# A hybrid decoder layer on one core: the SSM output in two parts, the pool fold in two kinds of PSUM banks, the norm weights first in the queue, the last rows by three engines

## The chip, the cores and the metric

The kernel runs on one core of one Trainium2 chip. The metric is the device time of one execution in microseconds. The core has a matrix engine (TensorE, PE), three other compute engines (VectorE or DVE, ScalarE or ACT, GpSimd or POOL) and a queue engine (SyncE, SP). All of them run their own instruction streams in order and wait for each other by semaphores. TensorE multiplies from SBUF into PSUM, which has eight banks here: two under the name mm and six under the name aux.

## The reference

One decoder layer: a normalised input goes through one projection, whose parts feed three mixers; each is gated, and an output projection with a norm is added to the input.

```python
h = rmsnorm(x, g_pre[i])                      # x: 2048 x 1024
proj = h @ w_in[i]                            # 1024 -> 2048
val, gate = proj[..., :MIX_W], proj[..., MIX_W:]
y_pool = pool_mixer(u_pool, w_pool[i], pool_scale[i])     # windows 2, 4, 8, 16; a 96x96 map per group
y_ssm = s5_mixer(u_ssm, ...)                  # 24 groups of 16 channels, 64 complex states each
y_att = memory_attention(q, mem, g_mem[i], w_kv[i])       # 4 heads, 256 memory tokens
y = jnp.concatenate([y_pool, y_ssm, y_att], axis=-1) * jax.nn.silu(gate)
out = y @ w_out[i]
x = x + rmsnorm(out, g_post[i])
```

The part of the state-space mixer that the change touches:

```python
bu = jnp.einsum('blgc,gnc->blgn', uf.astype(jnp.complex64), b_bar)
_, hs = lax.associative_scan(_ssm_combine, (lam_all, bu), axis=1)
y = jnp.einsum('blgn,gcn->blgc', hs, c_mat).real + d_skip.reshape(SSM_NG, SSM_GROUP) * uf
```

## The kernel before

All products are of float32 accuracy: each operand is split into a high and a low part (names ending in h and l), and a product is three matmuls (mm3, L163 to L165): high x high, high x low, low x high. The high part is a copy on ScalarE (L159), the low part a subtraction on VectorE or GpSimd (L160).

The run has these stages. Up to about 100 us x and the weights are loaded, the SSM input u is projected (pu) and stored, and keys and values of the memory are made. The rows of x are squared on ScalarE (L194, tile rs_x) and VectorE turns the sums into the norm factor rs_y (L170 to L198), which TensorE spreads to all partitions (rs_bc, L205). pool_fold multiplies the pool map into its columns of w_in ahead of use: eight pieces pf, each copied out by VectorE as wpo (L356) and stored; VectorE also copies out the projected u as us (L302). gpre, the norm weights, scales every split of x (L251, L252).

Then come two halves of the sequence, each with two chunks of 512 columns and 13 tasks (q, pool, gate): a task multiplies 128 columns of w_in with a chunk (pjq, pjp, pjg, L163 to L165) in an mm bank, and VectorE takes the product out times the norm factor (qf, up, gp). The first half runs from about 105 to 305 us, the second from about 345 to 505. Between them the splits of x for chunks 2 and 3 are made anew (xr is the load, xh and xl the split), and the weights that the first half has split are read back from DRAM (wq_h, wq_l and so on).

Between the tasks two queues of small steps are served, at a pace fixed by constants. One is the attention: scores psc, row maximum nb, exponentials pex, transposes ptp with their split pth and ptl, values po with lot and attn. The other is the SSM, in 12 blocks of two groups. For block b, ssm_build2 makes pr (a transpose, split into rh and rl) and pk (the short-range kernel, stored and read back as mraw, split into mh and ml). ssm_run1 multiplies the input (uh, ul) into pa, ScalarE swaps its halves (ax), VectorE and GpSimd rotate it (v), VectorE scans it (gg), rotates back (gs, h), and splits the states into hh and hl. ssm_run2 makes the output py of one aux bank: for each of two groups the near part, mh and ml times uh and ul, and the far part, oh and ol times hh and hl. ScalarE copies it out (ys) for the store. All these products sit in aux banks, and a new one has to wait until the reader of the bank's last content is done.

The order of instructions on each engine is set ahead of the run by a scheduler from the program's order and its own estimate of durations. From 505 us the GLU and the output projection (pout) run; the last 128 rows are done by out_last: three pieces of 512, 256 and 256 columns, squares on ScalarE, the reciprocal root oy on VectorE in small steps, the residual added in two halves (L1227), and a store on SP.

## Time and profile before

| | |
|---|---|
| median of the runs | 748.64 us (744.86, 748.64, 751.7) |
| profiled execution | 748.52 us, of which the span is 746.8 |
| mean granted clock of TensorE | 0.977 |
| TensorE busy | 711.5 us (95%) |
| VectorE busy | 498.8 us (67%) |
| ScalarE, GpSimd busy | 349.6 us, 354.0 us (47% each) |

The span is what the profiler's records cover; the rest of the time of the execution lies around it. Busy time is given for the whole span, and the stages differ much: a table of stages gives it for any stretch. A wait is the idle time of an engine ahead of an instruction, put down to what ended it. The granted clock is a share of TensorE's full clock of 2.4 GHz.

### The profile page before, as it was taken

What the parts mean: (1) busy time and instruction counts of PE and PEld (TensorE: products, weight loads), DVE (VectorE), ACT (ScalarE), POOL (GpSimd) and SP (SyncE); (2) the same over time, 40 slices, a digit from 0 to 9 for tenths busy, and PEclk for the clock granted to TensorE, in tenths of its full rate; (3) what the DMA queues carried; (4) which work ended last, traced back from release to release, by engine and by line L of the source; (5) the groups of instructions that cost most, each with busy time, mean ns of one, the idle gap of its engine ahead of it and who ended that gap; (6) DMA issues with size and microseconds to landing.
All of it is one profiled execution on the core that took longest, in us unless ns stands there. A gap on an engine that the chain in (4) does not pass through costs nothing.

```text
span 746.8 us, 10110 instructions
## 1 busy us (share of the span) xinstructions
PE 711.5 (95%) x3465; PEld 579.3 (78%) x3465; DVE 498.8 (67%) x865; ACT 349.6 (47%) x769; POOL 354.0 (47%) x311
## 2 busy tenths in 40 slices
PE   6999989998999799889999999999999999999996
PEld 5787768787878688667888888888877888888885
DVE  5699255689888887996887788648617963343324
ACT  5774662566565544354646555446633424121111
POOL 0058732768778476646948678103032621421121
PEclk9999989999999899899999999999999999999998
DMA  8998993333443366474232333387716453340331
GB/s 259 302 335 252 351 315 107 121 116 105 122 145 109 124 201 210 133 270 136 71 108 87 125 116 129 108 259 280 217 54 222 127 201 100 113 141 0 113 113 56
DMA packets 94978, 120.49 MB, mean 161 GB/s; under 512 B 31552, under 2 KB 62992, under 8 KB 94928
## 3 DMA queue, kind: packets, MB, share of 16 engines
q1 hardware_dynamic: 82032, 89.56, 37.8%
q10 hardware_dynamic: 12896, 30.30, 10.7%
q8 instruction: 27, 0.44, 0.2%
q14 instruction: 23, 0.19, 0.1%
HBM read 81.16 MB, written 38.68 MB: 160 GB/s over the span
## 4 chain that ended last, share of the span: by engine, by line
PE 67%; DVE 15%; DMA 8%; issue 4%; ACT 3%; POOL 2%; SPq 0%; ACTq 0%; DVEq 0%; POOLq 0%
PE pout L165 8%; PE pout L164 8%; PE pout L163 8%; PE pjg L163 6%; PE pjg L165 6%; PE pjg L164 6%; PE pz L163 2%; PE pz L164 2%; PE pz L165 2%; DMA xr<-in_xT_dram 2%; PE pjq L165 2%; PE pjq L163 2%; PE pjq L164 2%; DVE xl L252 2%; PE pjp L163 2%
## 5 line engine op out<-in xcount | busy, mean ns | idle before, releaser
L163 PE MATMUL pjg<-xh,wg_h 128*128 128x512 f32 x256 | 103.6, 405 | 0.0
L164 PE MATMUL pjg<-xl,wg_h 128*128 128x512 f32 x256 | 102.5, 400 | 0.0
L165 PE MATMUL pjg<-xh,wg_l 128*128 128x512 f32 x256 | 102.3, 400 | 0.0
L164 PE MATMUL pout<-wol,yh 128*128 128x512 f32 (+1 forms) x264 | 102.0, 386 | 0.0
L163 PE MATMUL pout<-woh,yh 128*128 128x512 f32 (+1 forms) x264 | 101.6, 386 | 0.0
L165 PE MATMUL pout<-woh,yl 128*128 128x512 f32 (+1 forms) x264 | 101.2, 387 | 0.0
L1213 POOL TENSOR_TENSOR ov<-ov,xres 128x1024 f32<-128x1024 f32 x15 | 36.7, 2446 | 127.6 <-DVE ov L1212 105.8
L1209 ACT ACTIVATE ov<-pout 128x512 f32<-128x512 f32 x30 | 17.9, 596 | 106.9 <-PE pout L165 83.9
L163 PEld LDWEIGHTS pjg<-xh,wg_h 128*128 128x128 f32 x256 | 48.7, 190 | 12.4 <-issue 1.2
L164 PEld LDWEIGHTS pout<-wol,yh 128*128 128x128 f32 x264 | 49.5, 188 | 10.9
L163 PEld LDWEIGHTS pout<-woh,yh 128*128 128x128 f32 x264 | 49.5, 188 | 10.9
L165 PEld LDWEIGHTS pout<-woh,yl 128*128 128x128 f32 x264 | 49.5, 188 | 10.9
L165 PEld LDWEIGHTS pjg<-xh,wg_l 128*128 128x128 f32 x256 | 48.7, 190 | 11.0
L164 PEld LDWEIGHTS pjg<-xl,wg_h 128*128 128x128 f32 x256 | 48.7, 190 | 10.5 <-issue 0.2
L160 POOL TENSOR_TENSOR yl<-yb,yh 128x512 fp32r<-128x512 f32 x20 | 27.2, 1395 | 59.4 <-ACT yh L159 59.4
L252 DVE SCALAR_TENSOR_TENSOR xl<-xr,gpre,xh 128x512 fp32r<-128x512 f32 x48 | 41.2, 874 | 16.4 <-ACT xh L251 15.8
L840 POOL TENSOR_TENSOR v<-v,ax 128x512 f32<-128x512 f32 x12 | 16.1, 1342 | 71.1 <-DVE ax L839 56.9
L251 ACT ACTIVATE xh<-xr,gpre 128x512 fp32r<-128x512 f32 x48 | 33.2, 714 | 26.5 <-DMA xr<-in_xT_dram 12.7
L163 PE MATMUL pu<-xh,wsh 128*128 128x512 f32 x96 | 38.5, 415 | 7.4 <-ACT wsh L159 5.9
L1181 DVE SCALAR_TENSOR_TENSOR ow<-ssq,ov 128x1 f32<-128x1 f32 x16 | 2.7, 168 | 55.5 <-ACT ov L1209 55.4
L163 PE MATMUL pjp<-xh,wp_h 128*128 128x512 f32 x96 | 38.7, 404 | 0.0
L164 PE MATMUL pu<-xl,wsh 128*128 128x512 f32 x96 | 38.4, 413 | 0.3 <-DVE xl L252 0.3
(299 smaller groups left out, 1915.0 us busy)
## 6 DMA issues: line engine op xcount, KB each, us to landing
xr<-in_xT_dram SPq DMA_DIRECT2D x32, 256.0 KB
rs_x<-in_x_dram SPq DMA_DIRECT2D x32, 256.0 KB
yd<-yt ACTq DMA_DIRECT2D x16, 512.0 KB
xres<-in_x_dram SPq DMA_DIRECT2D x16, 512.0 KB
out_dram<-ov SPq DMA_DIRECT2D x15, 512.0 KB
yb<-yd SPq DMA_DIRECT2D x20, 256.0 KB
wg_r<-in_w_in_dram SPq DMA_DIRECT2D x8, 512.0 KB
wsh<-wg_h ACTq DMA_DIRECT2D x8, 512.0 KB
```

Source lines behind the costliest of these rows:

```text
L160: sub.tensor_tensor(lo, src, hi.bitcast(F32), op=ALU.subtract)
L163: pe.matmul(ps, ahi, bhi, start=first, stop=False)
L164: pe.matmul(ps, ahi, blo, start=False, stop=False)
L165: pe.matmul(ps, alo, bhi, start=False, stop=last)
L251: act.activation(h, xr, AF.Copy, scale=gpre[:, k:k + 1])
L252: dve.scalar_tensor_tensor(l, xr, gpre[:, k:k + 1], h.bitcast(F32), op0=ALU.mult, op1=ALU.subtract)
L840: pool.tensor_tensor(v, v, ax, op=ALU.add)
L1181: dve.scalar_tensor_tensor(w, ssq[:, i:i + 1], 1.0 / D, v, op0=ALU.mult, op1=ALU.add)
L1209: act.activation(ov[:, HALVES[n]], ps[n], AF.Square, accum_out=ssq[:, n:n + 1])
L1213: pool.tensor_tensor(ov, ov, xr, op=ALU.add)
```

## The change

Four places are changed. The load of gpre is issued by SP instead of ScalarE, and stands first in SP's queue. The odd pieces of the pool fold go to aux banks, the even ones stay in mm banks. ssm_run2 is split: ssm_near stands where it stood, and ssm_far, with the copy ys and its stores, comes one step later, ahead of ssm_run1 of the next block; py stays open between them. The split of oh and ol goes along to the step of ssm_run1. In out_last the last two pieces are scaled by ScalarE, get the residual added on GpSimd and are stored by SP, and the first piece stays on VectorE and is stored from ScalarE's queue.

```diff
--- before.py
+++ after.py
@@ -139,7 +139,7 @@
 
 
     gpre = const.tile([P, KT], F32, name="gpre")
-    nc.scalar.dma_start(gpre, g_pre)
+    nc.sync.dma_start(gpre, g_pre)
     cs = const.tile([P, C_N], F32, name="cs")
     gmem = const.tile([P, KT], F32, name="gmem")
     warm = const.tile([P, 1], F32, name="warm")
@@ -349,7 +349,7 @@
                 dma(wt, w_in_poolT[:, :, r * P:(r + 1) * P])
 
                 def mms():
-                    ps = mm_bank(f"pf{r}", (P, POOL_W))
+                    ps = (aux_bank if r % 2 else mm_bank)(f"pf{r}", (P, POOL_W))
                     for g in range(4):
                         pe.matmul(ps[:, g * 96:(g + 1) * 96], wt[:, g, :], wp[:, g, :], start=True, stop=True)
                     wo = ev(f"wpo{r}", (P, POOL_W))
@@ -859,13 +859,19 @@
         split(hh, hl, h)
         o["hh"], o["hl"] = hh, hl
 
-    def ssm_run2(b, o):
+    def ssm_near(b, o):
+
+        py = o["py"] = aux_bank(f"py{b}", (P, 2, NJ))
+
+        for i in range(2):
+            mm3(py[:, i, :], o["mh"][:, i, :], o["ml"][:, i, :], o["uh"][:, i, :], o["ul"][:, i, :], i == 0, False)
+
+    def ssm_far(b, o):
+
         g0 = 2 * b
-        hh, hl = o["hh"], o["hl"]
-        py = aux_bank(f"py{b}", (P, 2, NJ))
+        hh, hl, py = o["hh"], o["hl"], o["py"]
         for i in range(2):
-            mm3(py[:, i, :], o["mh"][:, i, :], o["ml"][:, i, :], o["uh"][:, i, :], o["ul"][:, i, :], True, False)
-            mm3(py[:, i, :], o["oh"][:, i, :], o["ol"][:, i, :], hh[:, i, :], hl[:, i, :], False, True)
+            mm3(py[:, i, :], o["oh"][:, i, :], o["ol"][:, i, :], hh[:, i, :], hl[:, i, :], False, i == 1)
         ys = t2k(f"ys{b}", (P, 2, NJ))
         act.activation(ys, py, AF.Copy)
         for i in range(2):
@@ -878,20 +884,20 @@
         def call(*fs):
             def go():
                 for f, b in fs:
-                    if b < NB:
+                    if 0 <= b < NB:
                         f(b, ssm_state[b])
 
             ssm_q.append(go)
 
         call((ssm_input_load, 0), (ssm_build1, 0))
         call((ssm_build2, 0), (ssm_rotation, 0))
-        call((ssm_input_split, 0), (ssm_output_split, 0))
-        for b in range(NB):
+        call((ssm_input_split, 0))
+        for b in range(NB + 1):
             n = b + 1
-            call((ssm_run1, b), (ssm_kernel_load, b), (ssm_build1, n))
+            call((ssm_far, b - 1), (ssm_output_split, b), (ssm_run1, b), (ssm_kernel_load, b), (ssm_build1, n))
             call((ssm_kernel_split, b), (ssm_rotation, n))
             call((ssm_input_load, n))
-            call((ssm_run2, b), (ssm_build2, n), (ssm_input_split, n), (ssm_output_split, n))
+            call((ssm_near, b), (ssm_build2, n), (ssm_input_split, n))
 
 
     def q_split(ps, pr, c, qst):
@@ -1223,9 +1229,14 @@
             act.activation(sq[:, 0:cols.stop - cols.start], ps, AF.Square, accum_out=ssq[:, n:n + 1])
             dve.tensor_tensor(ov[:, cols], ps, w3["g"][:, cols], op=ALU.mult)
         r = out_rstd(c, tt, ssq, len(LAST))
-        for cols in HALVES:
-            dve.scalar_tensor_tensor(ov[:, cols], ov[:, cols], r, xr[:, cols], op0=ALU.mult, op1=ALU.add)
-            dma(out[rows, cols], ov[:, cols])
+        for cols in LAST[1:]:
+            st = t2k(f"st{cols.start}", (P, cols.stop - cols.start))
+            act.activation(st, ov[:, cols], AF.Copy, scale=r)
+            pool.tensor_tensor(st, st, xr[:, cols], op=ALU.add)
+            dma(out[rows, cols], st)
+        cols = LAST[0]
+        dve.scalar_tensor_tensor(ov[:, cols], ov[:, cols], r, xr[:, cols], op0=ALU.mult, op1=ALU.add)
+        store(out[rows, cols], ov[:, cols])
 
     HALVES = (slice(0, CH), slice(CH, D))
     LAST = (slice(0, CH), slice(CH, CH + 256), slice(CH + 256, D))
```

Behind line 860 the lines of the changed kernel are numbered 6 higher. What the change does to the order is shown at three places.

TensorE at SSM block 3, in the first half, before (pjg3_0_1 is a gate task on chunk 1, pr4 and pk4 belong to block 4):

```order
L165 MATMUL py3_2845<-hh3_2582,ol3_2498 128x256
L163 MATMUL py3_2845<-uh3_2493,mh3_2691 128x256
L164 MATMUL py3_2845<-ul3_2494,mh3_2691 128x256
L165 MATMUL py3_2845<-uh3_2493,ml3_2692 128x256
L163 MATMUL py3_2845<-hh3_2582,oh3_2497 128x256
L164 MATMUL py3_2845<-hl3_2583,oh3_2497 128x256
L165 MATMUL py3_2845<-hh3_2582,ol3_2498 128x256
L741 MATMUL pr4_2860<-ident_79,rt4_2594 128x128 x2
L163 MATMUL pjg3_0_1_2884<-xh1_4_860,wg3_0_h_2601 128x512
L164 MATMUL pjg3_0_1_2884<-xl1_4_861,wg3_0_h_2601 128x512
L165 MATMUL pjg3_0_1_2884<-xh1_4_860,wg3_0_l_2602 128x512
L750 MATMUL pk4_2867<-ox4_2589,rt4_2594 16x128 x2
```

and now, first the end of the near part with what follows it, then the far part:

```order
L163 MATMUL py3_2845<-uh3_2485,mh3_2691 128x256
L164 MATMUL py3_2845<-ul3_2486,mh3_2691 128x256
L165 MATMUL py3_2845<-uh3_2485,ml3_2692 128x256
L741 MATMUL pr4_2852<-ident_79,rt4_2592 128x128 x2
L750 MATMUL pk4_2859<-ox4_2587,rt4_2592 16x128 x2
L163 MATMUL pjg3_0_1_2872<-xh1_0_836,wg3_0_h_2599 128x512
L164 MATMUL pjg3_0_1_2872<-xl1_0_837,wg3_0_h_2599 128x512
```

```order
L165 MATMUL pjg3_0_1_2872<-xh1_7_878,wg3_0_l_2600 128x512
L163 MATMUL py3_2845<-hh3_2580,oh3_2551 128x256
L164 MATMUL py3_2845<-hl3_2581,oh3_2551 128x256
L165 MATMUL py3_2845<-hh3_2580,ol3_2552 128x256
L163 MATMUL py3_2845<-hh3_2580,oh3_2551 128x256
L164 MATMUL py3_2845<-hl3_2581,oh3_2551 128x256
L165 MATMUL py3_2845<-hh3_2580,ol3_2552 128x256
L163 MATMUL pa4_2930<-uh4_2868,rh4_2855 128x256
```

The six rows on hh, hl, oh and ol have moved 34 rows down, to just ahead of pa4, and pr4 and pk4 follow the near part directly. The attention's values po1_1_0 stand between the two pieces.

SP at the half change, where x is loaded anew and the split weights are read back, before:

```order
L116 DMA xr3_0_3536<-in_xT_dram 128x2x512
L116 DMA xr3_1_3546<-in_xT_dram 128x2x512
L116 DMA xr3_2_3560<-in_xT_dram 128x2x512
L116 DMA wq1_1_h_3548<-wsh1_1383 128x1024
L116 DMA wq1_1_l_3549<-wsl1_1384 128x1024
L116 DMA rs_b3_3580<-rsd_105 128x512
L116 DMA xr3_3_3570<-in_xT_dram 128x2x512
```

and now:

```order
L116 DMA xr3_0_3534<-in_xT_dram 128x2x512
L116 DMA xr3_1_3544<-in_xT_dram 128x2x512
L116 DMA wq1_1_h_3546<-wsh1_1379 128x1024
L116 DMA wq1_1_l_3547<-wsl1_1380 128x1024
L116 DMA rs_b3_3578<-rsd_105 128x512
L116 DMA xr3_2_3558<-in_xT_dram 128x2x512
L116 DMA xr3_3_3568<-in_xT_dram 128x2x512
```

The two tiles of wq1 have moved ahead of xr3_2, and xr3_2 stands behind them and rs_b3.

ScalarE from the output of block 0 to the swap ax of block 1, before:

```order
L159 ACTIVATE oh1_1743<-ox1_1487 128x256
L870 ACTIVATE ys0_1721<-py0_1708 128x512
L755 ACTIVATE kst1_1733<-pk1_1730 16x2x128
L934 ACTIVATE pex0_0_1_0_1673<-pex0_0_1_0_1673,ri0_0_1_0_1677 128x256 x2
L934 ACTIVATE pex0_0_1_1_1683<-pex0_0_1_1_1683,ri0_0_1_1_1687 128x256 x2
L964 ACTIVATE lot0_0_0_1769<-po0_0_0_1760 64x256
L119 DMA ysd_86<-ys0_1721 8x16x256 x2
L119 DMA kd1_1737<-kst1_1733 16x512
L997 ACTIVATE th0_0_1927<-gp0_0_1925 128x512
L964 ACTIVATE lot0_0_0_1769<-po0_0_0_1760 64x256
L831 ACTIVATE ax1_1806<-pa1_1799 64x512
L832 ACTIVATE ax1_1806<-pa1_1799 64x512
```

and now:

```order
L1003 ACTIVATE th0_0_1925<-gp0_0_1923 128x512
L970 ACTIVATE lot0_0_0_1757<-po0_0_0_1748 64x256
L876 ACTIVATE ys0_1791<-py0_1708 128x512
L831 ACTIVATE ax1_1804<-pa1_1797 64x512
L832 ACTIVATE ax1_1804<-pa1_1797 64x512
L119 DMA ysd_86<-ys0_1791 8x16x256
L970 ACTIVATE lot0_0_0_1757<-po0_0_0_1748 64x256
```

The copy ys0, which stood nine rows ahead of ax1, now stands directly ahead of it. In the same way ys1 to ys5 stand up to three rows ahead of ax2 to ax6, and there the split oh2 to oh6 stands next to them.

## Rows read from the trace of the kernel before

**Rows 1.** Table of stages: start:end us, length, busy us by engine, granted clock, DMA.

```profile
131.00:250.00 119.00, 111.51 (x611) 90.34 (x609) 101.08 (x142) 67.76 (x164) 91.80 (x77) 0.98 0.37 123
...
345.00:740.00 395.00, 392.85 (x1887) 321.14 (x1885) 230.34 (x446) 160.51 (x357) 150.74 (x119) 1.00 0.40 132
```

**Rows 2.** TensorE's waits over the whole run: us in total, times, longest.

```profile
PE py L164 <- DVE hl L160: 6.8, 5, 4.0
...
PE pf L354 <- DVE wpo L356: 4.7, 3, 3.2
...
PE pjq L163 <- DMA wq_h<-wsh: 2.0, 1, 2.0
...
PE py L163 <- ACT hh L159: 1.9, 1, 1.9
...
PE pjq L165 <- DMA wq_l<-wsl: 1.1, 2, 0.6
```

**Rows 3.** Timeline around the pool fold: start us, us, engine, line, operation.

```profile
98.69 1.03 DVE L302 COPY us<-pu 128x512 f32<-128x512 f32 x1 [6.71 <-ACT rs_x L194]
...
100.87 0.54 DVE L356 COPY wpo<-pf 128x384 f32<-128x384 f32 x1
...
105.39 0.77 PE L163 MATMUL pjq<-xh,wq_h 128*128 128x512 f32 x1
...
114.83 0.18 DVE L179 SCALAR_TENSOR_TENSOR rs_y<-rs_b,rs_y 128x16 f32<-128x16 f32 x1
...
117.17 1.05 PE L205 MATMUL rs_bc<-ident,rs_y 128*128 128x128 f32 x8
```

**Rows 4.** Table of stages, stretches with a low granted clock (PEclk).

```profile
101.20:108.00 6.80, 6.36 (x22) 5.64 (x23) 4.30 (x7) 5.25 (x17) 2.42 (x4) 0.50 1.04 386
...
212.60:217.30 4.70, 3.52 (x14) 2.96 (x13) 3.85 (x6) 1.87 (x7) 3.83 (x4) 0.64 0.10 41
...
246.60:254.80 8.20, 4.17 (x16) 3.25 (x16) 7.26 (x12) 3.30 (x9) 2.58 (x3) 0.58 0.51 185
...
309.40:316.30 6.90, 5.98 (x20) 4.58 (x19) 5.24 (x7) 1.87 (x4) 2.24 (x3) 0.51 0.58 181
```

**Rows 5.** Timeline, blocks 1, 2 and 3: ptl on VectorE, pk on TensorE.

```profile
181.38 1.29 DVE L160 TENSOR_TENSOR ptl<-ptp,pth 128x512 fp32r<-128x512 f32 x2
...
183.47 0.62 PE L750 MATMUL pk<-ox,rt 128*16 128x128 f32 x4
...
213.84 1.29 DVE L160 TENSOR_TENSOR ptl<-ptp,pth 128x512 fp32r<-128x512 f32 x2
...
217.46 0.62 PE L750 MATMUL pk<-ox,rt 128*16 128x128 f32 x4
...
251.29 1.29 DVE L160 TENSOR_TENSOR ptl<-ptp,pth 128x512 fp32r<-128x512 f32 x2
...
254.42 0.78 PE L750 MATMUL pk<-ox,rt 128*16 128x128 f32 x4
```

**Rows 6.** Timeline of ScalarE in block 0 and at the start of block 1.

```profile
155.71 0.61 ACT L870 ACTIVATE ys<-py 128x512 f32<-128x512 f32 x1
...
160.10 0.60 ACT L831 ACTIVATE ax<-pa 64x512 f32<-64x512 f32 x1 [0.40 <-PE pa L165]
```

**Rows 7.** Chain of waits at the half change: start us, us, what.

```profile
319.26 8.44 DMA wq_l<-wsl
```

**Rows 8.** Timeline of the first microseconds, ScalarE.

```profile
4.74 0.72 ACT L251 ACTIVATE xh<-xr,gpre 128x512 fp32r<-128x512 f32 x1 [2.05 <-DMA gpre<-in_g_pre_dram]
```

**Rows 9.** Timeline of the tail.

```profile
739.59 0.38 ACT L1223 ACTIVATE lsq<-pout 128x256 f32<-128x256 f32 x1 [2.33 <-PE pout L165]
...
742.35 1.41 DVE L1227 SCALAR_TENSOR_TENSOR ov<-ov,oy,xres 128x512 f32<-128x512 f32 x2
```

**Rows 10.** Groups by line and shape, GpSimd: busy us, mean ns of one, idle before.

```profile
L726 POOL TENSOR_TENSOR rt<-rt,cmbr 128x256 f32<-128x256 f32 x12 | 16.5, 1376 | 0.0
...
L725 POOL TENSOR_TENSOR cmbr<-Bim,YT__114 128x256 f32<-128x256 f32 x12 | 9.6, 803 | 0.0
```

## The prediction

> **What bounds the kernel now.** I read the table of stages first, then TensorE's waits, then the chain and the timeline at the places that the change touches. TensorE is the bound: from 345 to 740 us it is busy for 392.85 of 395 us at full clock, and in the middle of the first half (131 to 250 us) for 111.51 of 119 [rows 1]. A microsecond that TensorE gains before 345 us therefore reaches the end whole, since nothing behind it has idle time to give. The list of its waits says what can be gained [rows 2]: 6.8 us for hl in five places (the longest 4.0) and 1.9 for hh, both in the SSM output py, 4.7 for the evacuation wpo of the pool fold, and 2.0 + 1.1 for the reloaded weights wq_h and wq_l at the half change.
>
> To that comes the clock. Around the fold the granted clock is 0.50 over 6.8 us, and after the hl waits 0.64 over 4.7, 0.58 over 8.2 and 0.51 over 6.9 us [rows 4]; in each case TensorE had stood idle just before. Half clock is the lower of its two levels (1.2 against 2.4 GHz), so such a stretch loses its length times what is missing: 6.8 x 0.50 = 3.4 us at the fold, and 1.7 + 3.4 + 3.4 = 8.5 us behind hl. What the SSM part could give at the very most is 8.7 + 8.5 = 17.2 us. TensorE's waits end with a product of VectorE, though, and VectorE is busy for 101.08 of the 119 us [rows 1]: a near second limit.
>
> **The SSM output in two parts: 4.0 us gained (bounds 17.2 gained, 7 lost).** The near part (mh, ml times uh, ul) stays where all of py stood, the far part (oh, ol times hh, hl) goes to just ahead of pa of the next block. By the order of block 3 that is 34 rows of TensorE behind the near part, so the wait for hl is covered. But pr and pk of the next block now follow the near part directly, and pk needs the PSUM bank that the transposes ptp held, so it waits for VectorE's ptl; ptl still stands behind hl on VectorE. So I ask what is left if VectorE ends ptl no earlier than before. Then pk can begin when ptl ends [rows 5]: at block 1 at 181.38 + 1.29 = 182.67 against 183.47 (0.8 us sooner), at block 2 at 213.84 + 1.29 = 215.13 against 217.46 (2.3), at block 3 at 251.29 + 1.29 = 252.58 against 254.42 (1.8). That is 4.9 us, of which the six far matmuls that now come behind pk take back some: the stage from 345 us has 392.85 us for 1887 matmuls [rows 1], 0.21 apiece and mostly 512 columns wide; at half that width I estimate 0.11, so 3 x 6 x 0.11 = 2.0. Left are 2.9 us. VectorE's own idle time, 119 - 101.08 = 17.9 us [rows 1], lies partly behind products of TensorE and shrinks as these come sooner; I put 1.1 us on that, near the low end, because the row that decides (ptl behind hl) is the nearer one. Block 0 has no wait to lose, and block 5's is counted at the half change.
>
> The step also moves ys (the copy of py) and the split oh, ol. ys and its two stores on the ACT queue now stand just ahead of ax, which feeds the scan. ys takes 0.61 us, and ax waited 0.40 us for pa before it began [rows 6]; the far matmuls end six matmuls (about 0.7 us) before pa does, so ys fits under pa if ScalarE is free: zero, at most 0.6 for each block (the rival below). oh and ol wait for no product of TensorE: nothing. From 345 us on TensorE loses 2.15 us in all [rows 1], so there the split can gain next to nothing, and with the same slack it costs nothing. The change of the start flag has no instruction.
>
> **The half change: 1.5 us gained (0 to 4.8).** In SP's order the reload of wq1 (h and l) now stands ahead of xr3_2 instead of behind it. Before, its second half took 8.44 us from 319.26 to 327.70, and that ended the last wait of the stage [rows 7]. Issued a few us earlier it would take away the 2.0 + 1.1 us of the two weight waits [rows 2], and with them half of the 3.4 us of half clock of this stage could go as well, 4.8 in all. Against that, xr3_2 now queues behind those two weight tiles and rs_b3, and their splits xh, xl are on the same chain, so I take half of the 3.1 us and nothing of the rest.
>
> **The pool fold: 2.0 us gained (0 to 2.6).** With odd pieces in the six aux banks, pf no longer waits for the copy two pieces back. The last piece waits for the aux bank of us, which VectorE leaves at 98.69 + 1.03 = 99.72, and the first pjq for wpo in the mm bank, out at 100.87 + 0.54 = 101.41, instead of starting at 105.39 [rows 3]. By that alone the gain is 4.0 us, and with the clock (3.4) up to 7.4. It is capped, however: TensorE comes to rs_bc at 117.17, and rs_bc needs the last rs_y, which is ready at 114.83 + 0.18 = 115.01 [rows 3]; its chain begins when ScalarE has squared the last rows. No more than 117.17 - 115.01 = 2.2 us pass this point unless the squares end sooner; the copies' stores leave ScalarE's queue a little earlier, for which I add 0.4 to the bound. I take 2.0.
>
> **Norm weights first in the SP queue: 0 (0.5 either way).** gpre gates the first xh at 4.74 us [rows 8]. It moves ahead of all loads on SP, and every SP issue behind it comes one issue later. What the first chunk gains or loses is taken up by the same rs_y cap at 115 us, since the row squares hang on loads.
>
> **Last rows by three engines: 0.6 us lost (0.5 gained to 1.7 lost).** Before, VectorE writes both halves in 1.41 us from 742.35, the second ends at 743.76 [rows 9]. Now ScalarE copies two pieces of 256 columns with the scale (0.38 us for the like-sized square), so they are out at about 742.7 and 743.1, and GpSimd adds the residual. Its operations of 128x256 take 0.80 and 1.38 us in the mean of two lines [rows 10]: the second add ends at 742.7 + 1.6 = 744.3 or at 742.7 + 2.8 = 745.5, 0.5 or 1.7 behind. I take 0.8, nearer the first, whose inputs are as plain; the last store is half as large, for which I take 0.2 off. From 743.76 to the end of the span are 3.0 us; were a third of that saved by the smaller store, the tail would gain 0.5. Beside this VectorE's own step of 0.75 us (two SBUF inputs) runs at the same time as the adds. The Trainium skill ("SBUF — State Buffer", section "Who interferes with whom") says that a VectorE instruction with two SBUF inputs contends with a GpSimd instruction that reads SBUF; by it the tail would be about 0.75 us worse, and no row of before shows this pair alone.
>
> **Sum.** The profiled execution took 748.5 us, 1.7 us more than its span, and stands at the median of the runs (748.6). 748.5 - 4.0 - 1.5 - 2.0 + 0 + 0.6 = 741.6 us.
>
> **Rivals.** *All of it comes.* VectorE's idle time in the stage (17.9 us) falls along with TensorE's, ptl too comes sooner, and the far waits and their half clock go. For it: six hl and hh places are covered by some 30 rows of work; against it: VectorE is 85% busy there and ptl has the same instructions ahead of it. At two thirds of 17.2: 748.5 - 11.5 - 3.1 - 2.0 + 0.6 = 732.5 us.
>
> *Nothing but the fold.* VectorE is the real bound of the half: the wait goes from hl to the bank of pk and the half clock stays. Then 748.5 - 2.0 + 0.6 = 747.1 us.
>
> *Slower, by ys ahead of ax.* The chain pa, ax, v, gg, hl, ptl is the loop that paces a block. If ScalarE is late, ys (0.61) and the split oh (0.4, as the like-sized square in [rows 9]; next to ys in the order from block 2 on) push ax back in each of seven blocks of the first half. And py now holds its aux bank until ys has run; in the order psc of two attention units waits for ys, which it did not before. 7 x (0.6 + 0.4) = 7 us, one more short stretch of half clock 1.7, fold and half change nothing, tail 0.6: 748.5 + 9.3 = 757.8 us. It decides when ScalarE is still busy as the far part ends. Against it: ScalarE is busy for 67.76 of 119 us [rows 1] and idled ahead of ax in the row shown. By itself stands what the Trainium skill says ("PSUM — Partial Sum Buffer", "Summary: rules for kernel authors"): "Evacuate promptly". The change does the opposite with py, and by that rule this case is the outcome; the trace of before cannot show it, since py was emptied at once there.
>
> **Chances.** Forecast 0.40 (its own range 738 to 745), all of it 0.22, only the fold 0.27, slower 0.11. A measurement of this kernel can tell about 1% (7.5 us) from no change. Faster by over 1% (below 741.1): all of the second case and half of the forecast's, 0.43. Slower by over 1% (above 756.1): most of the last case, 0.10. The rest, 0.47, is within 1%. The range leaves out half of the slow case and some of the best: 731 to 753 us.
>
> **What the profile after would show.** The forecast is right if py no longer waits for hl or hh before 305 us, pk or pr wait for ptl or attn instead (3 to 6 us in all), the first pjq starts near 101.5 and rs_bc near 115, and the wait for wq_h is short. VectorE's busy share of the stage should rise above 85%. It is wrong on the good side if pk does not wait and no half clock is granted from 131 to 250 us; on the bad side if ax starts later behind pa than 0.1 us, if psc waits for ys, or if rs_y itself comes later.

## The result and the profile after

The changed kernel takes 754.71 us (median of 12 runs, 752.26 to 756.79) against 748.92 us for the kernel before (12 runs, 744.86 to 751.7): a ratio of 1.0082, interval 1.0065 to 1.0098. It is slower, by 5.8 us in the median; 741.6 us was forecast. The profiled execution took 752.26 us, of which the span is 750.0 (746.8 before). It is the shortest of the 12, so the trace shows 3.2 us of the loss and understates the rest.

TensorE's waits in the changed kernel (us in total, times, longest), to be laid beside [rows 2]:

```profile
PE pk L750 <- DVE ptl L160: 7.5, 2, 4.5
...
PE pjq L163 <- DMA wq_h<-wsh: 5.5, 1, 5.5
PE pr L741 <- POOL ss L818: 2.1, 1, 2.1
PE pr L741 <- POOL ur L783: 2.1, 1, 2.1
...
PE pz L163 <- ACT gh L159: 1.7, 1, 1.7
...
PE py L164 <- DVE hl L160: 0.8, 1, 0.8
...
PE pr L741 <- DVE attn L971: 0.6, 1, 0.6
```

The wait for hl fell from 6.8 to 0.8 us, that for hh went, and that for wpo went. In their place stand 7.5 us of pk for ptl and 4.8 us of pr: both wait for the bank of a product that VectorE has still to read. Where the list names GpSimd, pr waited for attn, which empties the bank of po: in block 3 below attn ends at 244.71 + 0.43 = 245.14 and pr starts at 245.28, 0.14 us later; in blocks 1 and 2 attn ends at 176.47 and 206.92 and pr starts 0.14 us behind it as well. New too are 1.7 us for gh, in the GLU, and 3.5 us more for wq_h.

The table of stages (start:end, length, busy us by engine, granted clock, DMA), first the stretches of [rows 1]:

```profile
131.00:250.00 119.00, 105.89 (x570) 84.93 (x568) 108.09 (x137) 66.21 (x161) 91.61 (x77) 0.95 0.35 116
345.00:740.00 395.00, 391.07 (x1872) 318.54 (x1873) 229.36 (x447) 159.21 (x354) 149.96 (x117) 1.00 0.41 133
```

and the stretches that ran at half clock, to be laid beside [rows 4]:

```profile
177.65:181.05 3.40, 3.40 (x12) 2.04 (x10) 3.40 (x8) 2.47 (x11) 0.00 (x0) 0.50 0.03 7
211.80:215.20 3.40, 3.40 (x9) 2.72 (x9) 2.32 (x6) 2.84 (x11) 0.67 (x1) 0.50 0.22 89
245.90:256.10 10.20, 5.93 (x16) 4.33 (x17) 8.34 (x14) 5.84 (x18) 2.52 (x3) 0.50 0.53 193
324.40:331.20 6.80, 4.41 (x10) 3.02 (x11) 6.01 (x8) 2.19 (x4) 6.20 (x6) 0.50 0.95 359
```

From 131 to 250 us TensorE does 570 matmuls where it did 611. VectorE is busy longer there for fewer instructions (108.09 us for 137, against 101.08 for 142): some last longer, such as hl in block 3 with 1.75 us, 0.69 before. The stretch of half clock at the fold is gone, but the four new ones last 23.8 us and cost 11.9 us at 0.50, as much as the four of [rows 4] did (3.4 + 1.7 + 3.4 + 3.4); the kernel before had a fifth, from 326.49 to 329.90 us, that those rows leave out (1.7 us more). So the half clock as a whole cost no more than before, but it fell in other places. Each new stretch begins during or just behind a wait of pr, pk or wq_h.

Where the lead goes is read from the starts of the same tasks in the timelines (the first matmul of each; us). The last two columns are of experiments below.

| task | before | after | build later (e13) | last far at once (e14) |
|---|---|---|---|---|
| first pjq, behind the fold | 105.39 | 99.76 | 99.58 | 100.71 |
| first pjg of chunk 1 | 156.85 | 150.53 | 150.66 | 151.56 |
| second pjg of chunk 0 | 185.33 | 183.34 | 180.24 | 184.43 |
| third pjp of chunk 1 | 205.74 | 207.23 | 202.06 | 208.38 |
| fifth pjg of chunk 0 | 258.29 | 261.48 | 250.47 | 262.56 |
| first pjp of the second half | 349.12 | 350.11 | 344.49 | 350.71 |
| first pz of the GLU | 509.56 | 510.21 | 505.75 | 511.17 |
| pz behind the wait for ov, late in the GLU | 560.90 | 563.93 | 557.08 | 562.50 |

So at the fold the change leads by 5.6 us, and at the first pjg of chunk 1 by 6.3. In blocks 1 to 3 it loses 9.5 us and is 3.2 behind; the half change gives 2.2 back, the second half 0.3, and the GLU takes 2.4. Some small products (po, pa) stand on the other side of such a start in the other kernel, so a difference holds to about 1 us. From 131 to 260 us TensorE's waits add up to 13.4 us after and 8.1 before, and at a granted clock of 0.93 and 0.96 some 3.9 us more of full clock are missing (0.03 x 129): 9.2 us together, close to those 9.5.

The timeline of TensorE in block 3 shows the loss (start us, us, engine, line, operation; in brackets the idle time before, and what the profile says ended it). Before:

```profile
250.71 0.58 PE L164 MATMUL py<-hl,oh 128*128 128x256 f32 x1 [4.03 <-DVE hl L160]
...
252.59 0.63 PE L741 MATMUL pr<-ident,rt 128*128 128x128 f32 x2
```

and after:

```profile
242.94 0.28 PE L165 MATMUL py<-uh,ml 128*128 128x256 f32 x1
245.28 0.41 PE L741 MATMUL pr<-ident,rt 128*128 128x128 f32 x2 [2.06 <-POOL ur L783]
250.17 1.04 PE L750 MATMUL pk<-ox,rt 128*16 128x128 f32 x4 [4.47 <-DVE ptl L160]
251.14 0.80 PE L163 MATMUL pjg<-xh,wg_h 128*128 128x512 f32 x1
251.74 0.63 PE L164 MATMUL pjg<-xl,wg_h 128*128 128x512 f32 x1
```

and VectorE beside it, where each row follows the one before at once:

```profile
244.71 0.43 DVE L971 TENSOR_TENSOR attn<-po,lot 64x256 f32<-64x256 f32 x1
245.17 1.23 DVE L160 TENSOR_TENSOR wg_l<-wg_r,wg_h 128x1024 fp32r<-128x1024 f32 x1
246.31 1.75 DVE L160 TENSOR_TENSOR hl<-h,hh 128x512 fp32r<-128x512 f32 x1
247.99 0.68 DVE L1008 SCALAR_TENSOR_TENSOR th<-th,gp 128x512 f32<-128x512 f32 x1
248.70 0.69 DVE L1009 SCALAR_TENSOR_TENSOR yt<-s,th 128x512 f32<-128x512 f32 x1
249.42 1.29 DVE L160 TENSOR_TENSOR ptl<-ptp,pth 128x512 fp32r<-128x512 f32 x2
```

After the change, behind the near part (its last matmul at 242.94) come pr and pk, and both wait: 2.06 and 4.47 us, 6.5 in all, where TensorE had waited 4.0 for hl. Behind them stands the whole next projection task, 24 matmuls that depend on none of this and cannot pass. When it starts it runs at 0.43 us a matmul in place of 0.23. ptl itself came a little earlier than before: 249.42 against 251.29 [rows 5].

The same place in blocks 1 and 2 (after; to be laid beside the pk rows of [rows 5]):

```profile
176.61 0.41 PE L741 MATMUL pr<-ident,rt 128*128 128x128 f32 x2 [2.10 <-POOL ss L818]
...
179.94 1.04 PE L750 MATMUL pk<-ox,rt 128*16 128x128 f32 x4
...
207.06 0.41 PE L741 MATMUL pr<-ident,rt 128*128 128x128 f32 x2 [0.57 <-DVE attn L971]
...
211.19 0.63 PE L750 MATMUL pk<-ox,rt 128*16 128x128 f32 x4 [3.02 <-DVE ptl L160]
```

pk starts 3.5, 6.3 and 4.2 us sooner than before. That is the odd point of this result: the instruction for which everything was counted came sooner, and the tasks came later.

### The profile page after: what moved, and what is told of

It reads as the page before. It is cut to its first block, busy times and chain, and to the rows that moved or that the text cites. A ratio compares the mean times of both kernels' runs of the same rounds, so it can differ in the third digit from the quotient of the medians.

```text
span 750.0 us, 10127 instructions
## 1 busy us (share of the span) xinstructions
PE 710.1 (95%) x3465; PEld 577.3 (77%) x3465; DVE 505.0 (67%) x864; ACT 349.2 (47%) x771; POOL 360.0 (48%) x313
## 4 chain that ended last, share of the span: by engine, by line
PE 59%; DVE 19%; DMA 10%; ACT 5%; issue 5%; POOL 1%; ACTq 0%; SPq 0%; POOLq 0%; DVEq 0%
PE pout L165 7%; PE pout L164 7%; PE pout L163 7%; PE pjg L163 6%; PE pjg L164 5%; PE pjg L165 5%; DVE gg L843 2%; DMA xr<-in_xT_dram 2%; PE pz L163 2%; PE pz L164 2%; PE pz L165 2%; DMA rs_x<-in_x_dram 2%; DVE xl L252 2%; DMA yr<-ysd 1%; DMA mr<-in_memT_dram 1%
## 5 line engine op out<-in xcount | busy, mean ns | idle before, releaser
L163 PE MATMUL pjg<-xh,wg_h 128*128 128x512 f32 x256 | 104.1, 406 | 0.6 <-DVE up L1033 0.6
L164 PEld LDWEIGHTS pjg<-xl,wg_h 128*128 128x128 f32 x256 | 48.7, 190 | 10.2 <-issue 0.2
L164 PE MATMUL pjp<-xl,wp_h 128*128 128x512 f32 x96 | 39.1, 407 | 0.0
L165 PE MATMUL pjp<-xh,wp_l 128*128 128x512 f32 x96 | 38.9, 406 | 0.0
```

The lines of the kernel that those rows point to most:

```text
L163: pe.matmul(ps, ahi, bhi, start=first, stop=False)
L164: pe.matmul(ps, ahi, blo, start=False, stop=False)
L165: pe.matmul(ps, alo, bhi, start=False, stop=last)
```

## The experiments

Ratios are to the kernel before, measured on the same chip between the same rounds, with the 95% interval. The median of that kernel was 747.23 to 748.74 us in the four sets.

**Which part loses: the parts alone and in pairs.** e1 is the changed kernel with the SSM output whole again (parts of the edit; ssm_run2 is that of the kernel before):

```diff
...
-        call((ssm_input_split, 0))
-        for b in range(NB + 1):
+        call((ssm_input_split, 0), (ssm_output_split, 0))
+        for b in range(NB):
...
-            call((ssm_far, b - 1), (ssm_output_split, b), (ssm_run1, b), (ssm_kernel_load, b), (ssm_build1, n))
+            call((ssm_run1, b), (ssm_kernel_load, b), (ssm_build1, n))
...
-            call((ssm_near, b), (ssm_build2, n), (ssm_input_split, n))
+            call((ssm_run2, b), (ssm_build2, n), (ssm_input_split, n), (ssm_output_split, n))
```

> The changed kernel with the SSM output whole again (ssm_run2 as before); fold, norm weights and last rows as changed. Theory A (the split costs): TensorE reached rs_bc 5.8 us earlier in the changed kernel and lost 9.1 us between the first tasks and block 4, at new waits of pr and pk; without the split the 5.8 us should stay to the end, 748.9 - 5.8 + 0.2 = about 743 us, and pk and pr should not wait. Theory B (VectorE is the bound of the first half, so any lead is eaten there, split or not): about 748 us, with longer waits of py for hl. Theory C (the split is harmless and the GLU stage, 2.2 us, and the reload are what lost): above 750 us.

Measured: 749.0 us, 1.0025 (1.0008 to 1.0041). Without the split most of the loss is gone: 1.0082 against 1.0025, so the split costs 0.57% here, some 4.3 us. But the fold's gain does not show in the time either. Its waits say where it went:

```profile
PE py L164 <- DVE hl L160: 8.9, 4, 4.0
...
PE py L163 <- ACT hh L159: 3.8, 1, 3.8
```

12.7 us for hl and hh, 8.7 before [rows 2]: TensorE arrives earlier and waits longer.

e2 is the split alone, in the kernel before (the change's hunks on ssm_near, ssm_far and the queue, and no other).

> The kernel before with the split of the SSM output alone. Theory A: the split loses some 5 to 9 us in blocks 1 to 3 and gains 4 at block 5, so 751 to 756 us, with pk waiting for ptl and pr for attn in the place of py for hl. Theory B: no change, about 748.9 us, the waits only change their names.

Measured: 747.88 us, 1.0005 (0.9987 to 1.0023). The wait for hl fell to 0.7 us, pr waited 4.9 us for attn and 0.7 more, pz 1.5 us for gh, and pk not at all. One wait became another, and the time stayed.

e3 is the fold alone:

```diff
-                    ps = mm_bank(f"pf{r}", (P, POOL_W))
+                    ps = (aux_bank if r % 2 else mm_bank)(f"pf{r}", (P, POOL_W))
```

> The kernel before with the odd pieces of the pool fold in aux banks, nothing else. By my prediction the gain is capped at about 2 us by rs_y; the changed kernel showed rs_bc 5.8 us earlier. If the fold alone does this, rs_bc starts at about 111.4 us here, and by theory A the time is about 743 us; by theory B rs_bc is early and the time is about 748 us. If rs_bc is at 115 us or later, another part of the change (gpre ahead in the queue) made rs_y early.

Measured: 746.26 us, 0.9984 (0.9965 to 1.0004), a gain at the edge of what these rounds can tell. In its trace rs_bc starts at 112.17 and the first pz at 503.78, 5.0 and 5.8 us earlier than before, so there the lead lasts to the GLU; but this execution (742.79 us) is the shortest of its 12.

e6 moves the load of gpre alone:

```diff
-    nc.scalar.dma_start(gpre, g_pre)
+    nc.sync.dma_start(gpre, g_pre)
```

> The kernel before with the norm weights first in SP's queue, nothing else. The kernel with fold, norm weights and last rows (without the split) was 0.4% above the fold alone. If the norm weights are the cause of that, this is 2 to 3 us above the kernel before; if it is the last rows or chance of the order, no change.

Measured: 745.6 us, 0.9975 (0.9963 to 0.9988): 1.9 us gained, which neither case expected.

e12 is the change of the last rows alone (the hunk in out_last).

> The kernel before with the last rows by three engines alone. My prediction put 0.6 us of loss on it (0.5 gained to 1.7 lost); the trace of the changed kernel has the end of the span 7.5 us behind the last matmul against 7.3. So 0.2 to 0.6 us above the kernel before, which the measurement cannot tell from nothing. If it is the last rows that made the kernel without the split slow, 2 to 4 us above.

Measured: 748.61 us, 0.9996 (0.998 to 1.0011): nothing.

e11 is fold and gpre together, without the split and with the old tail.

> The fold and the norm weights together, no split, last rows as before. Alone they were 0.998 and 0.9975 of the kernel before. If they add up, 0.994 to 0.997, about 744 to 746 us, faster than both kernels. Order by chance in the first half can cost as much as that again: then about 748 us.

Measured: 749.78 us, 1.001 (0.9994 to 1.0027), with 8.7 us of waits for hl and 3.1 for hh. Two edits that gain a little alone gain nothing together. Why is not shown: in this trace rs_bc starts at 113.99, later than with the fold alone (112.17), so there was no second lead to lose.

e5 is split and fold, without the other two.

> The split and the fold together, without the move of the norm weights and with the last rows as before. Alone the split was 1.0005 and the fold 0.998 of the kernel before. If the two spoil each other (the lead of the fold brings TensorE to the new bank waits of pr and pk before VectorE is there), this is 752 to 755 us and carries nearly the whole loss. If the parts simply add up, it is about 747 us, and the loss of the whole change lies in the norm weights or the last rows.

Measured: 755.71 us, 1.0107 (1.0091 to 1.0123), with the same waits as the whole change (pk 7.5; pr 2.1, 2.1 and 0.5). The whole loss is in this pair, while its members alone measure 1.0005 and 0.9984. So it is an interaction, and the question was of what. The traces show one thing that the fold does to the order: in block 2 pk stands behind 22 of the 24 matmuls of its projection task in e2 and behind 3 in e5, in block 3 behind 5 and behind none.

**Is VectorE's amount of work the bound?** e7 and e8 leave out 13 low parts of weights in the first half, in the kernel before and in the changed one (parts of the edit); the high part takes their place, so the matmuls and DMAs stay the same in number and size, and the values differ.

```diff
...
-        split(wh, wl, wr)
+        act.activation(wh, wr, AF.Copy)
...
-            dma_later(spill[1], wl.bitcast(F32))
-        return wh, wl
+            dma_later(spill[1], wh.bitcast(F32))
+        return wh, wh
```

> The kernel before, in which the low part of the 13 tasks' weights is not made in the first half: VectorE's subtraction is left out and the high part stands in for it in the products and the spill (so the products of both halves use the high part twice). VectorE loses about 13 x 1.3 to 2.6 = 17 to 30 us of work between 105 and 305 us. If VectorE bounds the first half (theory B), the waits of py for hl go and the time falls by 8 to 15 us; if the waits are a matter of the place of py in the order, they stay and the time falls by less than 3 us.

> The changed kernel with the same work left out on VectorE. By theory B the waits of pk for ptl and of pr for attn go as well, the lead of the fold (5.8 us) lasts, and this is 2 to 5 us faster than the kernel before with the same cut (2.2 us of the lead are lost in the GLU stage). If pr and pk wait for another reason than VectorE's lag, it is slower than that kernel, as the changed kernel is without the cut.

Measured: e7 746.89 us, 0.9987 (0.9971 to 1.0002); e8 753.54 us, 1.0077 (1.0053 to 1.01). From 131 to 250 us VectorE is busy for 95.89 us in e7 (101.08 before) and for 99.91 us in e8 (108.09 in the changed kernel); the hl waits are 9.0 us in e7 (6.8 before), and in e8 the pk waits are 6.5 us (7.5 in the changed kernel) and those of pr 1.0 (4.8). 5 to 8 us less work on VectorE shorten some waits and leave the time where it was: its amount alone is not the bound. The other reading, that it counts when ptl and attn are reached, is what the next runs try.

**Is it the place of pr and pk?** e4 lets the far part stay in its own step, behind pr and pk (the main line of the edit; the step of ssm_run1 and the loop are those of the kernel before):

```diff
...
-            call((ssm_near, b), (ssm_build2, n), (ssm_input_split, n))
+            call((ssm_near, b), (ssm_build2, n), (ssm_far, b), (ssm_input_split, n), (ssm_output_split, n))
```

> The changed kernel with the far part in the same step as the near part, behind pr and pk of the next block, in place of one step later; oh and ol split where they were before. The far products keep little cover (pr and pk alone). If the loss comes from py holding its bank up to the next step, this loses less than the changed kernel (about 748 us); if it comes from pr and pk following the near part so closely that they wait for the banks of ptl and attn, the waits of pk stay and the time is about 754 us; if hl's wait was the cost, it returns beside them and the time is above 755 us.

Measured: 755.84 us, 1.012 (1.0094 to 1.0145). Both kinds of wait are there (hl 6.2 us; pr 3.5 and 2.1, and pk for ptl 2.3), as the last of the three cases has it, and the wait for gh is not.

e10 is the split alone, as e2, with the build handed to the scheduler 30 places earlier; e9 is the whole change with it 30 places later. The edit of e9 (e10 has +30 for -30):

```diff
+    def build2_late(b, o):
+        with tc.high_priority(offset=-30):
+            ssm_build2(b, o)
...
-            call((ssm_near, b), (ssm_build2, n), (ssm_input_split, n))
+            call((ssm_near, b), (build2_late, n), (ssm_input_split, n))
```

> The split alone (which was as fast as the kernel before), with pr and pk at a higher priority, so that they and the near part stand about as early as in the changed kernel: in block 2 the near part at the end of pjp2_0_0 with pk 5 matmuls into pjp2_0_1 (9 and 13 later without this), in block 3 pk ahead of all of pjg3_0_1. Fold, norm weights and last rows are as before. Theory C: the loss appears without the fold, 752 to 756 us, with the waits of pk for ptl. If it takes the lead of the fold to lose (the two really interact), it stays at 747 to 749 us.

> The changed kernel with pr and pk (ssm_build2) at a lower priority for the scheduler, so that they stand behind 15 more projection matmuls in blocks 2 and 3 (in pjp2_0_1 and pjg3_0_1) while the near part and the transposes keep their places. Theory C (place): the change loses because pr and pk ask for the banks of attn and ptl early in a projection task, and the rest of that task, 21 to 24 matmuls or about 5 us, is queued behind the wait. Then the waits of pk for ptl (7.5 us) and of pr (4.7 us) shrink to below 3 us together and the time falls by 4 to 7 us, to 748 to 751 us. Theory B (VectorE is late whatever the place) or a loss elsewhere: the wait goes to po or far and the time stays at 753 to 756 us.

Measured: e10 758.06 us, 1.0113 (1.0092 to 1.0135); e9 754.57 us, 1.0074 (1.0049 to 1.01). The split that cost nothing in e2 costs 1.1% when pr and pk come early, without the fold. Its waits are those of the change:

```profile
PE pk L750 <- DVE ptl L160: 4.2, 2, 3.3
...
PE pr L741 <- POOL ur L783: 3.1, 1, 3.1
...
PE pr L741 <- DVE attn L975: 1.9, 1, 1.9
```

pk stands behind 5 matmuls of its task in block 2 (22 in e2) and behind none in block 3 (5 in e2); in the changed kernel these are 3 and none. The near part has moved up too, to both sides of pr. So an earlier place of the build is enough for the loss. The way back was less clear. In e9 pk stands behind 19 matmuls of its task in blocks 2 and 3, no pk row is left in the waits and 2.1 us of pr, below the 3 us of theory C, and the fifth pjg of chunk 0 starts at 254.79 in place of 261.48. But the median did not fall, against that theory. In the trace the GLU lost 4.8 us (first pz at 506.12, the pz behind the wait for ov at 562.21: 56.1 us, 51.3 before); there the granted clock is 0.90 from 533 to 550 us around this wait:

```profile
537.55 0.73 PE L163 MATMUL pz<-gh,wgh 128*128 128x512 f32 x2 [2.44 <-ACT gh L159]
```

And e9's other runs were 1.5 to 6.8 us longer than the profiled one (750.15 us), of which no trace tells.

**The place and the GLU apart.** e13 is e9 with the build 60 places later. In blocks 2 and 3 pr and pk then stand behind all 24 matmuls of the task and behind the far part, and the GLU's order is that of the kernel before.

```diff
...
+        with tc.high_priority(offset=-60):
+            ssm_build2(b, o)
...
```

e14 leaves the build where the change has it, and runs the far part of the last block alone in its own step:

```diff
-        for b in range(NB + 1):
+        for b in range(NB):
...
+        ssm_q[-1] = (lambda go: lambda: (go(), ssm_far(NB - 1, ssm_state[NB - 1])))(ssm_q[-1])
```

e16 gives the split of ptp priority over other ready work:

```diff
-            split(pth[:, o], ptl[:, o], ptp)
+            with tc.high_priority(offset=HP):
+                split(pth[:, o], ptl[:, o], ptp)
```

> The changed kernel whole, but the second state's build (the step that ends in the pr and pk matmuls) is handed to the scheduler 60 places late, so that pr and pk of blocks 2 and 3 stand behind the far part, and the order in the gated stage is that of the kernel before again. Theory (the place of pr and pk in TensorE's queue makes the loss, the gated stage's wait for gh the rest): 745 to 751 us, ratio 0.995 to 1.002, no pk wait over 1 us, no pz wait for ACT gh over 1 us. Rival (the two-part sum costs by itself, by its additional instructions on VectorE, ScalarE or GpSimd, wherever it stands): 753 to 756 us, ratio 1.005 to 1.011.

> The changed kernel whole, but the far part of the last block stands in the last block's own step, not a step later; the first half's order is the changed kernel's. Theory (the gated stage's wait for gh comes from that last far part and is worth the 2.2 us that the stage lost): 751 to 753.5 us, ratio 1.003 to 1.007, the pz wait for ACT gh gone, pk waits for ptl unchanged at 7 us. Rival (that wait is hidden by a later one, the whole loss stands in blocks 1 to 3): 754 to 756 us, ratio 1.007 to 1.010, with the gh wait gone all the same.

> The changed kernel whole, but the split of ptp into pth and ptl is given the high priority that hides an instruction from the queue's tail: VectorE takes it ahead of other ready work. Theory (pk waits 7 us because ptl stands behind other instructions in VectorE's queue, and the projection matmuls behind pk wait with it): pk's wait for ptl under 3 us in all and 748 to 752 us, ratio 0.998 to 1.004. Rival (ptl is late because its chain pa, h, hl, ptp is, or the wait goes to the bank of po in its place): pk plus pr waits stay above 7 us and the time 753 to 757 us, ratio 1.006 to 1.011.

Measured: e13 746.34 us, 0.9966 (0.9948 to 0.9985); e14 751.73 us, 1.0046 (1.0031 to 1.0061); e16 753.87 us, 1.0072 (1.0046 to 1.0099).

e13 has every edit of the change and is faster than the kernel before. TensorE's waits in it:

```profile
PE py L164 <- DVE hl L160: 6.5, 5, 1.9
...
PE py L165 <- DVE ml L160: 2.5, 3, 1.3
...
PE pjq L163 <- DMA wq_h<-wsh: 1.4, 1, 1.4
...
PE pk L750 <- DVE ptl L160: 0.2, 1, 0.2
```

and its table of stages (the columns as above), with the changed kernel's next:

```profile
131.00:260.00 129.00, 122.66 (x659) 98.59 (x657) 111.94 (x154) 76.29 (x187) 92.72 (x80) 0.99 0.40 131
```

```profile
131.00:260.00 129.00, 115.72 (x606) 92.61 (x605) 113.39 (x148) 72.04 (x179) 92.52 (x79) 0.93 0.35 115
```

The waits for hl are back to 6.5 us, but in five pieces of at most 1.9 us. Of them 2.8 us lie between 131 and 260 us, where all of TensorE's waits come to 6.1 us (13.4 in the changed kernel) and the granted clock is 0.99 in place of 0.93. 659 matmuls are done there in place of 606. Block 3 in e13 shows how the wait came to be short:

```profile
243.85 0.40 PE L165 MATMUL pjg<-xh,wg_l 128*128 128x512 f32 x1
244.09 0.27 PE L163 MATMUL py<-hh,oh 128*128 128x256 f32 x1
246.00 0.39 PE L164 MATMUL py<-hl,oh 128*128 128x256 f32 x1 [1.64 <-DVE hl L160]
...
246.70 0.38 PE L741 MATMUL pr<-ident,rt 128*128 128x128 f32 x2
247.33 0.41 PE L750 MATMUL pk<-ox,rt 128*16 128x128 f32 x2 [0.25 <-DVE ptl L160]
```

The task's last matmul (243.85) is done when TensorE meets the first wait of the block; after hl, pr does not wait and pk waits 0.25 us.

e14 removes the gh wait and 0.36% of the 0.82%, about 2.7 us, with the pk waits unchanged at 7.5 us. So the GLU's loss is worth 2.7 us by itself. Between e14 and e13 lies the place of the build, 1.0046 to 0.9966: 0.8%, or 6 us, if nothing else that e13 moves counts. The two together are more than the whole loss; the rest is then the gain that had been hidden.

e16 did not do what it meant. In block 3 VectorE took ptl at 254.59 us, still behind wg_l, hl, th and yt and 4.3 us behind the end of attn (250.25), as in the changed kernel (249.42 and 245.14; the whole trace of e16 runs some 5 us later there); pk waited 7.3 us. Whether a ptl that really goes first would end the wait stays open.

## Why the prediction was wrong

**What bounds the kernel: right.** TensorE's time gained in the first half does reach the end: in the table of starts e13 leads by 4.6 us at the start of the second half's pjp and by 3.8 through the GLU, and its span is 3.6 us shorter. One sentence was wrong: that the slack from 345 us on makes the split free there. The far part of the last block, a step later, delays gh and cost 2.7 us (e14).

**The split, 4.0 us gained: the step that failed.** The prediction asked when pk can begin, took ptl's end for it, and booked 0.8 + 2.3 + 1.8 us of earlier pk as TensorE's gain. pk did begin earlier, by more than that, and the split cost 4.3 us in place of gaining 4.0 (the whole change at 1.0082, without the split at 1.0025). TensorE is in order, and in the kernel before part of its work stood ahead of the wait for ptl: in block 3 pk came behind 15 matmuls of its projection task, 12 ahead of the near part and 3 behind pr. In the changed kernel none stands ahead and 24 stand behind; in block 2 it is 3 in place of 18. At 0.23 us apiece 15 matmuls are 3.5 us of cover: TensorE comes to the wait that much sooner and stands idle, 6.5 us in block 3 in place of 4.0. VectorE sets the time here in both kernels (TensorE waits for hl before and for ptl after), so an earlier pk with less work done ahead of it is no gain. What should have been counted was the idle time of TensorE ahead of pr and pk, and what is queued behind it. The prediction did look for waits of pr and pk, 3 to 6 us in all, but gave them no price in the sum; they took 12.3 us (7.5 and 4.8).

With more cover than before (e13, 24 matmuls in both blocks), the change with the split is 0.6%, 4.4 us, faster than the one without: e13 at 0.9966 against e1 at 1.0025. That this is near the 4.0 forecast is luck, since the order is another and e13 moves more rows than the build's. One reading was late as well: the row of ptl is two instructions, and in the trace after pk starts 0.05 us behind the end of the first (250.12), not of the second, so each of the three pk could have been called 0.6 us sooner. And the half clock from 309.4 us on, 3.4 us of the 8.5 put down to hl, begins behind a wait of 1.8 us for ml, which the split does not touch.

**The fold, 2.0 us gained, capped by rs_y: the cap is there, its time is not fixed, and the gain was eaten.** The rows behind the fold, after:

```profile
98.95 1.03 PE L354 MATMUL pf<-wp,wpt 96*128 96x96 f32 x8
99.76 0.47 PE L163 MATMUL pjq<-xh,wq_h 128*128 128x512 f32 x1
...
111.39 2.05 PE L205 MATMUL rs_bc<-ident,rs_y 128*128 128x128 f32 x16 [0.66 <-DVE rs_y L179]
```

```profile
95.65 1.05 DVE L302 COPY us<-pu 128x512 f32<-128x512 f32 x1 [4.23 <-ACT rs_x L194]
...
111.16 0.17 DVE L179 SCALAR_TENSOR_TENSOR rs_y<-rs_b,rs_y 128x16 f32<-128x16 f32 x1
```

TensorE starts pjq 5.6 us earlier, without half clock (101.2 to 108 us: 1.00 in place of 0.50), and does meet the cap, for 0.66 us. But rs_y is ready at 111.33 and not at 115.01 [rows 3], 3.7 us earlier, and the copies us come 3.0 earlier. How much of that the fold did is not shown: in the six traces without it rs_y is ready between 112.2 and 115.0 us, in the eleven with it between 110.7 and 115.9. The first pjq starts at 104.1 in the mean of the six and at 101.3 in that of the eleven, so the 5.6 us of this one pair are about 2.7 in the mean, and the first rs_bc gains 3.3. A time read from one trace was too sharp a bound, in either direction. With the split the lead was lost in front of pr and pk; without it, behind hl and hh in the traces of e1 and e11, while that of e3 keeps it.

**The half change, 1.5 us gained: it did not come.** SP issues the second wq_h at 318.57 us, as before (318.61), since it stands behind loads of xr that wait for their buffers:

```profile
312.50 6.02 SPq L116 DMA_DIRECT2D xr<-in_xT_dram  x3
318.57 0.80 SPq L116 DMA_DIRECT2D wq_h<-wsh  x1
```

In e13 the same issue comes at 310.28 and the wait is 1.4 us: the load follows the lead of the tasks, not its rank among its neighbours. The 2.2 us that this stage gives back in the table are mostly clock: 6.8 us of half clock (from 324.4) in place of 10.2 (from 309.4 and 326.5), 1.7 us.

**gpre, 0: a little too small.** The first xh starts at 4.59 us in place of 4.74 [rows 8]; alone the edit measures 1.9 us, more than the 0.5 allowed, by a way that the traces do not show plainly.

**The tail, 0.6 us lost: 0.2 in the trace, none in the time (e12).** From the last square to the end of the span 7.38 us, 7.21 before [rows 9]:

```profile
742.62 0.38 ACT L1229 ACTIVATE lsq<-pout 128x256 f32<-128x256 f32 x1 [2.33 <-PE pout L165]
...
745.37 0.91 ACT L1234 ACTIVATE st<-ov,oy 128x256 f32<-128x256 f32 x2 [2.28 <-DVE oy L1199]
745.38 0.75 DVE L1238 SCALAR_TENSOR_TENSOR ov<-ov,oy,xres 128x512 f32<-128x512 f32 x1
745.96 1.43 POOL L1235 TENSOR_TENSOR st<-st,xres 128x256 f32<-128x256 f32 x2 [7.96 <-ACT st L1234]
```

GpSimd's two adds take 1.43 us, 0.72 each, under both rows of [rows 10]; they end 0.6 us later than VectorE's halves did, and the two small stores give 0.4 back. The Trainium skill ("SBUF — State Buffer", section "Who interferes with whom") let one fear 0.75 us here; VectorE's step (0.75 us) and the adds share only 0.17 us, so no run tests the rule.

**The slower rival.** It ended on the right side by another mechanism than the one priced. Its sign is there: ax follows pa's end by 1.7 us in block 2 (183.50 to 185.22), since ys (184.29) and the split oh (184.79) stand ahead. But in e13 ax follows pa by 2.45 us in the same block (186.68 to 189.13), and e13 is faster than the kernel before; no psc waited for ys. The sentence "Evacuate promptly" that was quoted with it (the Trainium skill, "PSUM — Partial Sum Buffer", section "Summary: rules for kernel authors") holds of other banks than py's: those of ptp and po, whose readers on VectorE were late when pk and pr asked for them.

**The chances.** Those of a time faster by over 1% add up to 0.22 + 0.20 = 0.42, not 0.43.

**Open.** Why e9, whose trace has no pk wait and 19 matmuls ahead of pk, gained nothing in the median; it speaks against the place of pr and pk as the whole cause. How much of the effect of e10 and e13 comes from other moves, since an offset in the scheduler moves more rows than those of the build. And the traces are of single executions, those of the changed kernel, e3, e5, e8, e9 and e10 of the shortest of their runs, so a difference of 2 or 3 us between two of them can be chance.

## What to carry to other kernels

When an edit removes a wait on an in-order engine, list what stood between the old place and the next instruction that can wait: that work was cover, and an instruction that moves ahead of it takes its wait out into the open, with everything queued behind it. Price such an instruction by its idle time and its queue, not by its own start. A gain made upstream can end in the next wait downstream, and an edit in one place can move the scheduler's order in another, so test an edit together with its neighbours as well as alone: here two harmless edits (1.0005 and 0.9984) made 1.0107 together, and a later place for one step turned the whole change from 1.0082 into 0.9966. A bound on a gain that is read from one trace should be read from a second one too.

## What the runs showed of the hardware that was not expected

The clock cost about as much as the waits, between e13 and the changed kernel. From 131 to 260 us TensorE waits 6.1 us in e13, at most 1.6 at a time, and is granted 0.99; in the kernel before 8.1 us, once 4.0, and 0.96; in the changed kernel 13.4 us, once 4.5, and 0.93. From e13 to the changed kernel that makes 7.3 us more of waits and some 8 us less of full clock (0.06 x 129). Whether the length of the single wait counts beside the sum is not shown: e10 waits 13.0 us there, at most 3.3 at a time, and is granted 0.96; e2 waits 8.7 us, once 4.9, and is granted 0.97. And a VectorE with 5 to 8 us less to do (e7, e8) did not change the time, though in the trace of e8 the waits of this stage fell from 13.4 to 9.4 us.
